# The second layer's MLP output as seven block products in place of eight (Strassen), for three quarters of its hidden width

## The chip, the cores and the metric

One core of one Trainium2 chip. The metric is the device time in microseconds of one execution, median of the runs shown.

## The reference

A decoder trunk of two layers, 512 tokens of width 1024, in float32. Each layer mixes tokens (three mixers fed by one input projection) and then channels. The change is in the channel mixing of the second layer and the final norm:

```python
h2 = rms_norm(x, norm2_w[l]) * (1.0 + sc2) + sh2
x = x + g2 * (jnp.square(jax.nn.relu(h2 @ w_up[l])) @ w_down[l])
...
return rms_norm(x, final_norm_w)
```

w_up is 1024 x 4096, w_down 4096 x 1024. g2 is one number per output column.

## The kernel before, in words

The residual x lies in eight tiles xt[m], 128 of the 1024 columns on the partitions, the 512 tokens along the free axis. A matrix product is made of three matmuls on values split in two (mm3, lines 199 to 201): high times high, and the two mixed products. A split (lines 192 and 193, 469 and 470) is a ScalarE cast to fp32r, the high part, and a VectorE subtraction, the low part.

The work is a list of jobs (class Job). A job computes output columns for all tokens in PSUM banks of 128x512 and is cut into pieces of four blocks of 128 rows of the weights. For a piece, emit_split (line 448) loads 128x1024 weights into raw by SP's queue and splits them into wH and wL; emit_mm (line 474) issues the matmuls with the weights' 128x128 blocks as the stationary operand and the activations, 128x512, as the moving one. A job of two output blocks has two pieces of 24 matmuls. At a job's end its evac reads the PSUM banks. run (line 513) puts the jobs in order: it splits the pieces ahead of the one in work (two held at a time) and adds up estimated times of TensorE and VectorE, by which it slips in the mixers' streams; in the second layer's MLP there are no streams. This order is that of the program text; buffers and the final order on each engine are worked out for the whole program when it is compiled, with splits and evacs marked as of high priority.

The MLP goes in four quarters qt of the hidden width. In each, four jobs up{qt}{mp} compute Relu and square (lines 1491, 1492) and split the result into uH and uL; then four jobs dn{qt}{mp} multiply by w_down, and evac_dn adds the result, times g2, to xt (line 1504). In the first quarter the first two up jobs are paired: their weights are kept and the tokens go in two halves of 256. In the last quarter the last two dn jobs are paired too. There, evac_dn also turns each xt[m] into token order (to_tokens, lines 1453 to 1458: a transpose on TensorE, a square with its sum on ScalarE, a product with the final norm's weight on VectorE) and, after the last block, final (lines 1461 to 1473) computes the factor of each token (rstd_cols, lines 360 to 368), scales and stores 256 KB for each half of the columns of 128 tokens.

Of the kernel before, what the change touches and what calls it, by code (L numbers as in the profile page):

```python
# [10 lines left out]
F32 = mybir.dt.float32  # L11
# [72 lines left out]
class Job:  # L84
# [11 lines left out]
    def pieces(self):  # L96
        return [Piece(self, k0, self.step, k0 == 0, k0 + self.step >= self.nk) for k0 in range(0, self.nk, self.step)]
# [9 lines left out]
def paired(fin, a, b):  # L107

    a.fin = b.fin = fin
    a.left = b.left = 2  # L110
    ps = a.pieces() + b.pieces()
    for p in ps:
        p.keep = True
    return [Unit(p, c) for c in HALVES for p in ps]

# [35 lines left out]
def tile_trunk(ctx: ExitStack, tc: tile.TileContext, io, out, depth=DEPTH):  # L151
# [7 lines left out]
    pa = ctx.enter_context(tc.tile_pool(name="pa", bufs=26))  # L159
# [7 lines left out]
    def tmp():  # L167
        return tf.tile([P, T], F32, name="tmp", tag="tmp")
# [13 lines left out]
    def tr_bank():  # L182
        return psp.tile([P, T], F32, name="tr", tag="tr", bufs=2)
# [53 lines left out]
    def fixed(n):  # L237
        used[0] += n
        return slab[:, used[0] - n:used[0]]
# [151 lines left out]
    class SumSq:  # L391
        def __init__(self):
            self.acc = None
            self.kept = {}
# [52 lines left out]

    def emit_split(p):
        j = p.job
        w = sum(n for _, n in j.cols)  # L450
# [23 lines left out]
    def emit_mm(u, ks):  # L474
        p, c = u.p, u.c
        j = p.job
        if j.ps is None:
            if j.pre is not None:
                j.pre()
            j.ps = [(j.bank[i] if j.bank else acc_bank)() for i in range(len(j.ms))]  # L480
# [32 lines left out]
    def run(items, ahead=2, step=2):  # L513
# [43 lines left out]
        while True:  # L557
# [56 lines left out]
            w = (u.c.stop - u.c.start) / T  # L614
# [27 lines left out]
    def layer(l, lys):  # L642
# [790 lines left out]

        w_up = io["w_up"][l].rearrange("(k p) c -> p k c", p=P)
        w_dn = io["w_down"][l].rearrange("(k p) c -> p k c", p=P)
        if last:
            xw = [pa.tile([P, 4, P], F32, name="xw", tag="pa") for _ in range(8)]
            sqs = fixed(32).rearrange("p (a b) -> p a b", a=4)
            s4 = fixed(4)
            r4 = fixed(4)  # L1440
            q4 = fixed(4)
            fwb = [pa.tile([P, T], F32, name="fwb", tag="pa") for _ in range(2)]
            for i in range(2):
                sync.dma_start(fwb[i], io["final_norm_w"][i * T:(i + 1) * T].rearrange("(o d) -> o d", o=1).broadcast_to([P, T]))
        else:
            yield Stream(fin, "next", ada(l + 1, "next", [2, 3, 0, 1, 4, 5, 8, 9, 6, 7, 10, 11], pa, "pa", 2.0))
        ss = SumSq()

        def to_tokens(m, c):
            tbs = range(c.start // P, c.stop // P)  # L1450
            pt = tr_bank()
            for tb in tbs:
                pe.transpose(pt[:, tb * P:(tb + 1) * P], xt[m][:, tb * P:(tb + 1) * P], ident)
            q = tmp()
            for tb in tbs:
                act.activation(q[:, tb * P:(tb + 1) * P], pt[:, tb * P:(tb + 1) * P], AF.Square,
                               accum_out=sqs[:, tb, m:m + 1])
                dve.tensor_mul(xw[2 * tb + m // 4][:, m % 4, :], pt[:, tb * P:(tb + 1) * P],
                               fwb[m // 4][:, m % 4 * P:(m % 4 + 1) * P])

        def final(c):
            t = slice(c.start // P, c.stop // P)
            s_, r_, q_ = s4[:, t], r4[:, t], q4[:, t]
            dve.tensor_reduce(out=s_, in_=sqs[:, t, :], op=ALU.add, axis=mybir.AxisListType.X)
            rstd_cols(s_, r_, q_)
            for tb in range(t.start, t.stop):
                for i in range(2):
                    o = xw[2 * tb + i]
                    if i:
                        act.activation(o, o, AF.Identity, scale=r4[:, tb:tb + 1])  # L1470
                    else:
                        dve.tensor_scalar(o, o, r4[:, tb:tb + 1], None, op0=ALU.mult)
                    sync.dma_start(o2[tb * P:(tb + 1) * P, i * T:(i + 1) * T], o.rearrange("p m c -> p (m c)"))

        def dn_pre():
            exp_ln_set()
            if not last:
                lys[l + 1] = begin(l + 1)
                scale_of(l + 1, lys[l + 1]["A1"], M_SC1, "norm1_w")

        for qt in range(4):
# [19 lines left out]
            for mp in range(4):  # L1501
                def evac_dn(i, ps, c=ALL, mp=mp, qt=qt):
                    m = 2 * mp + i
                    dve.scalar_tensor_tensor(xt[m][:, c], ps[:, c], mod[l][:, M_G2 + m:M_G2 + m + 1], xt[m][:, c],  # L1504
                                             op0=ALU.mult, op1=ALU.add)
                    if qt == 3:
                        if last:
                            to_tokens(m, c)
                            if m == NK - 1:
                                final(c)  # L1510
                        else:
                            ss.add(xt[m], c, m)
                            if m == NK - 1:
                                norm1(l + 1, lys[l + 1], ss, c)
# [5 lines left out]
                                 need=["next"] if end and not last else ["ada.11"], pre=dn_pre if end else None))  # L1520
# [79 lines left out]
```

## Time and profile before

| | us |
|---|---|
| median of three runs | 1988.61 (1986.53 to 1992.06) |
| the profiled execution | 1988.82 |
| its span, first to last instruction | 1987.1 |
| TensorE busy in the span | 1949.8 |
| VectorE busy | 1277.8 |
| ScalarE busy | 871.6 |

The engines are PE (TensorE's matmuls), PEld (its weight loads, which overlap them), DVE (VectorE), ACT (ScalarE), POOL (GpSimd) and SP (the queue that issues the DMAs). A busy time is the union of an engine's instructions; a matmul's end is modelled, so of matmuls the distance between starts counts. The second layer's MLP goes from about 1625 us to the end of the span.

### The profile page before, as it was taken

The page shows a single profiled execution, that of the slowest core. Times are in us where ns is not written, and L with a number is a line of the kernel's source. Part 1 is how long each engine was busy: PE and PEld are TensorE (multiplying, and loading weights), DVE is VectorE, ACT ScalarE, POOL GpSimd, SP SyncE. Part 2 cuts the span into 40 slices and gives each one's busy share as a digit, 9 for nine tenths or more (in the row PEclk, how much of TensorE's full clock was granted, in tenths as well). Part 3 has the DMA queues.
Part 4 walks back from the last instruction along what each step waited for, and adds up shares of the span by engine and source line. Part 5 has one row for each costly group of instructions (what it writes and reads, how often), then busy time and mean ns, then how long its engine had stood idle before and what let it go on. Part 6 is the DMA issues. An engine that isn't in the chain of part 4 may idle for free.

```text
span 1987.1 us, 26736 instructions
## 1 busy us (share of the span) xinstructions
PE 1949.8 (98%) x9940; PEld 1613.1 (81%) x9940; DVE 1277.8 (64%) x2368; ACT 871.6 (44%) x1562; POOL 94.9 (5%) x135
## 2 busy tenths in 40 slices
PE   7998999999999999999999999999999999999998
PEld 5787777788888988888897787778888898888887
DVE  4799768967846986333578985687575572333334
ACT  4453626733534534142545445384343354233243
POOL 0110210100000000000001101001000000000000
PEclk9999999999999999999999999999999999999999
DMA  9864353552444694333425433425233422333321
GB/s 288 222 168 131 107 153 108 156 188 87 136 127 142 223 371 161 95 103 98 118 86 139 113 103 90 118 70 151 67 104 108 156 95 96 96 96 96 95 96 43
DMA packets 249623, 258.30 MB, mean 130 GB/s; under 512 B 33828, under 2 KB 208212, under 8 KB 249492
## 3 DMA queue, kind: packets, MB, share of 16 engines
q1 hardware_dynamic: 248912, 256.45, 42.3%
q8 instruction: 78, 1.28, 0.3%
q14 instruction: 53, 0.43, 0.1%
q10 hardware_dynamic: 356, 0.14, 0.0%
q0 software_dynamic: 224, 0.00, 0.0%
HBM read 232.81 MB, written 6.42 MB: 120 GB/s over the span
## 4 chain that ended last, share of the span: by engine, by line
PE 89%; DVE 5%; DMA 2%; issue 1%; ACT 1%; POOL 1%; SPq 0%; ACTq 0%; POOLq 0%; DVEq 0%
PE acc L199 25%; PE acc L201 25%; PE acc L200 25%; PE qk L225 2%; PE po L1001 1%; PE tr L992 1%; DVE wL L470 1%; PE po L907 1%; PE tr L894 1%; DVE sc L823 1%; PE qk L1204 1%; DVE m L822 1%; DMA araw<-in_ada_w_dram 1%; PE po L201 1%; PE po L200 1%
## 5 line engine op out<-in xcount | busy, mean ns | idle before, releaser
L199 PE MATMUL acc<-aH,wH 128*128 128x512 f32 x1544 | 613.6, 398 | 10.6 <-DVE paL L193 5.3
L201 PE MATMUL acc<-aH,wL 128*128 128x512 f32 x1544 | 606.7, 393 | 0.9 <-DVE wL L470 0.8
L200 PE MATMUL acc<-aL,wH 128*128 128x512 f32 x1544 | 606.5, 393 | 0.0
L469 ACT CAST wH<-raw 128x1024 fp32r<-128x1024 f32 (+2 forms) x290 | 295.2, 1026 | 289.5 <-PE acc L200 250.5
L470 DVE TENSOR_TENSOR wL<-raw,wH 128x1024 fp32r<-128x1024 f32 (+2 forms) x290 | 343.3, 1199 | 16.0 <-ACT wH L469 8.3
L199 PEld LDWEIGHTS acc<-aH,wH 128*128 128x128 f32 x1544 | 291.4, 189 | 72.8 <-DVE paL L193 6.1
L201 PEld LDWEIGHTS acc<-aH,wL 128*128 128x128 f32 x1544 | 291.0, 188 | 62.5 <-DVE wL L470 2.1
L200 PEld LDWEIGHTS acc<-aL,wH 128*128 128x128 f32 x1544 | 291.6, 189 | 57.6 <-issue 0.7
L199 PE MATMUL acc<-uH,wH 128*128 128x512 f32 x448 | 174.9, 390 | 0.0
L201 PE MATMUL acc<-uH,wL 128*128 128x512 f32 x448 | 174.6, 390 | 0.0
L200 PE MATMUL acc<-uL,wH 128*128 128x512 f32 x448 | 174.3, 389 | 0.0
L193 DVE TENSOR_TENSOR uL<-tmp,uH 128x512 fp32r<-128x512 f32 x64 | 43.9, 691 | 189.2 <-ACT uH L192 189.2
L1491 ACT ACTIVATE tmp<-acc 128x512 f32<-128x512 f32 x60 | 35.3, 592 | 220.0 <-PE acc L201 220.0
L1504 DVE SCALAR_TENSOR_TENSOR x<-acc,slab,x 128x512 f32<-128x512 f32 (+1 forms) x64 | 43.8, 716 | 128.7 <-PE acc L201 128.7
L343 DVE SCALAR_TENSOR_TENSOR aacc<-araw,slab,aacc 128x512 f32<-128x512 f32 x140 | 104.0, 749 | 5.7 <-DMA araw<-in_ada_w_dram 4.1
L200 PEld LDWEIGHTS acc<-uL,wH 128*128 128x128 f32 x448 | 84.1, 188 | 17.4
L201 PEld LDWEIGHTS acc<-uH,wL 128*128 128x128 f32 x448 | 84.1, 188 | 17.4
L199 PEld LDWEIGHTS acc<-uH,wH 128*128 128x128 f32 x448 | 84.1, 188 | 17.1
L882 DVE TENSOR_TENSOR_SCAN tmp<-tmp 128x512 f32<-128x512 f32 (+1 forms) x64 | 52.5, 826 | 21.5 <-ACT tmp L875 21.4
L675 POOL TENSOR_TENSOR tmp<-tmp,slab 128x512 f32<-128x512 f32 (+1 forms) x20 | 31.6, 1581 | 719.5 <-DVE tmp L674 708.6
L1312 DVE SCALAR_TENSOR_TENSOR tmp<-tg,acc 128x512 f32<-128x512 f32 x16 | 11.0, 685 | 67.0 <-PE acc L201 67.0
L822 DVE MAX8 m<-sc 128x8 f32<-128x256 f32 (+2 forms) x96 | 52.8, 552 | 1.2 <-POOL sc L800 0.2
(307 smaller groups left out, 3022.1 us busy)
## 6 DMA issues: line engine op xcount, KB each, us to landing
araw<-in_ada_w_dram SPq DMA_DIRECT2D x192, 256.0 KB, 5.4
raw<-in_w_in_dram SPq DMA_DIRECT2D x96, 512.0 KB, 4.1
raw<-in_w_up_dram SPq DMA_DIRECT2D x64, 512.0 KB, 4.6
raw<-in_w_down_dram SPq DMA_DIRECT2D x64, 512.0 KB, 4.6
raw<-in_w_in_dram SPq DMA_DIRECT2D x56, 256.0 KB, 4.4
acb<-acd SPq DMA_DIRECT2D x32, 256.0 KB, 4.6
raw<-in_w_br_ssd_dram SPq DMA_DIRECT2D x16, 512.0 KB, 4.5
raw<-in_w_out_dram SPq DMA_DIRECT2D x16, 512.0 KB, 4.2
```

Source lines behind the costliest of these rows:

```text
L193: dve.tensor_sub(L, src, H)
L199: pe.matmul(ps, a[0], b[0], start=start, stop=False)
L200: pe.matmul(ps, a[0], b[1], start=False, stop=False)
L201: pe.matmul(ps, a[1], b[0], start=False, stop=stop)
L225: pe.matmul(ps, q[hh][:, cq], k[n][hh][:, ck], start=n == 0, stop=n == 1)
L343: dve.scalar_tensor_tensor(a, raw, cs[:, k:k + 1], a, op0=ALU.mult, op1=ALU.add)
L469: act.copy(H[:, :w], src)
L470: dve.tensor_sub(L[:, :w], src, H[:, :w])
L822: dve.max(out=m8, in_=sc[tb])
L882: dve.tensor_tensor_scan(out=nv, data0=nv, data1=nv, initial=1.0, op0=ALU.mult, op1=ALU.bypass)
L1491: act.activation(r, ps, AF.Relu)
L1504: dve.scalar_tensor_tensor(xt[m][:, c], ps[:, c], mod[l][:, M_G2 + m:M_G2 + m + 1], xt[m][:, c], op0=ALU.mult, op1=ALU.add)
```

## The change

The second layer's MLP gets a function of its own, last_mlp; the first layer keeps the old code. Its weights are now the moving operand: a class Rows, derived from Job, has pieces of two blocks of 128 rows and 512 columns, and an output tile is 128 tokens by 512 columns. The hidden width goes in four quarters of eight blocks, taken as four pairs (e = 0, 1).

In the first three quarters the product is made by blocks: the tokens in two halves of 256, the hidden blocks by e, the output columns in two halves d. Seven products (1, 2, 6, 7, 5, 4, 3 in this order) replace eight. The four weight quadrants R[e, d] (128x2048 each) are loaded by DMA during the quarter's up stage; their sums are made in place on VectorE (t3 during the up stage, t2, t1 and t4 ahead of their products), each over 128x1024. The sums of activations (S) are made by VectorE at the end of each pair of up blocks, and they and the plain blocks are split: seven tiles of 128x512 a pair. A product has two token tiles of four blocks, two pieces of 12 matmuls; its evac adds each PSUM bank to the accumulators y (product 1 to two of them, product 6 to one of these), by a ScalarE copy where an accumulator is new. y[1] to y[4] take the tag at, y[5] and y[7] the tag acb; both are kinds of buffers of the mixers, as are those of R (yH, yL), of the rows of g2 and the norm's weight (tg, cbt) and of xtok (x).

During the first quarter's up stage x is turned into token order (32 transposes, eight ScalarE copies) and stored; it is loaded again in the last quarter's up stage, where so_far(0) and so_far(1) combine the accumulators, multiply by g2 and add x, 13 VectorE operations of 128x512 each. behind is a ScalarE copy of one column that keeps a load from starting before something else is done.

The last quarter is plain: job p0 for the first 512 output columns, four token tiles at once; job p1 for the others, one token tile after another over weights that are kept split (in the buffers of h2), each with its evac, its final and its two stores.

```diff
@@ pool
-    pa = ctx.enter_context(tc.tile_pool(name="pa", bufs=26))
+    pa = ctx.enter_context(tc.tile_pool(name="pa", bufs=28))
@@ beside emit_split and emit_mm, which call these for a Rows job
+    def split_form(p):
+        j = p.job
+        src = j.form(p.k0 // 2)
+        if p.keep:
+            p.H, p.L = ([ap_.tile([P, T], F32R, name=n, tag=n) for _ in range(p.nk)] for n in ("aH", "aL"))
+            with tc.high_priority():
+                for k in range(p.nk):
+                    split(src[:, k * T:(k + 1) * T], p.H[k], p.L[k])
+            return
+        H, L = (wp.tile([P, 1024], F32R, name=n, tag=n)[:, :p.nk * T] for n in ("wH", "wL"))
+        with tc.high_priority():
+            split(src, H, L)
+        p.H, p.L = ([X[:, k * T:(k + 1) * T] for k in range(p.nk)] for X in (H, L))
+
+    def product(u):
...
+        for i in range(u.c.start, u.c.stop):
+            if i not in j.ps:
+                j.ps[i] = psp.tile([P, T], F32, name="dn", tag="dn", bufs=4)
+            for k in range(p.nk):
+                kk = p.k0 + k
+                a = [X[:, i * P:(i + 1) * P] for X in j.lhs(kk)]
+                mm3(j.ps[i], a, (p.H[k], p.L[k]), kk == 0, kk == j.nk - 1)
+            if p.last:
+                with tc.high_priority():
+                    j.evac(i, j.ps[i])
...
@@ last_mlp
+            def plus(key, i, src):
+                if (key, i) not in y:
+                    y[key, i] = at_whole() if key < 5 else tf.tile([P, T], F32, name="acb", tag="acb", bufs=6)
+                    act.copy(y[key, i], src)
+                else:
+                    dve.tensor_add(y[key, i], y[key, i], src)
...
+            def evac_plain(d):
+                def f(tb, ps):
+                    t = tmp()
+                    dve.tensor_mul(t, ps, rowb["g", d])
+                    dve.tensor_add(xf[tb, d], xf[tb, d], t)
+                    squares(tb, d)
+                    if d == 0:
+                        dve.tensor_mul(xf[tb, d], xf[tb, d], rowb["f", d])
+                    else:
+                        final(tb, d)
+                return f
...
+            for n in (4, 4, 4, 4):
+                first, end = g0 == 0, g0 + n == 16
...
+                        split(r1[:, 0:V], aH, aL)
+                        split(r2, bH, bL)
+                        dve.tensor_add(S[0], r1[:, V:], r2[:, V:])
+                        dve.tensor_sub(S[1], S[0], r1[:, 0:V])
+                        split(c_, cH, cL)
+                        dve.tensor_sub(S[2], r1[:, 0:V], r1[:, V:])
+                        dve.tensor_sub(S[3], r2[:, 0:V], S[1])
+                        split(d_, dH, dL)
...
+                def fetch(e, d, h, R=R, us=us, g0=g0, n=n):
...
+                    behind(R[e, d, h], us["r", 0, 0])
+                    sync.dma_start(r,
+                                   w_dn[:, e, g0 + 2 * h:g0 + 2 * h + k, d * T:(d + 1) * T])
+
+                def t3(h, R=R):
+                    dve.tensor_sub(R[0, 1, h], R[1, 1, h], R[0, 1, h])
+
+                def t2(h, R=R):
+                    dve.tensor_add(R[0, 0, h], R[0, 1, h], R[0, 0, h])
+                    return R[0, 0, h]
+
+                def t1(h, R=R):
+                    dve.tensor_sub(R[0, 1, h], R[1, 1, h], R[0, 0, h])
+                    return R[0, 1, h]
+
+                def t4(h, R=R):
+                    dve.tensor_sub(R[0, 0, h], R[1, 0, h], R[0, 0, h])
+                    return R[0, 0, h]
...
+                def evac_of(m):
+                    def f(i, ps):
+                        for a in {1: (1, 2), 6: (1,)}.get(m, (m,)):
+                            plus(a, i, ps)
+                    return f
...
+                prods = [(1, raw_(0, 0), "a11"), (2, raw_(1, 0), "a12"), (6, t2, "s2"), (7, raw_(0, 1), "s3"),
+                         (5, t1, "s1"), (4, t4, "a22"), (3, raw_(1, 1), "s4")]
+                yield from add([Rows(f"p{m}.{g0}", n, form, lhs(a), 2, evac_of(m)) for m, form, a in prods])
@@ layer
         if last:
...
+            yield from last_mlp()
+            return
```

## Rows read from the trace of the kernel before

**Rows 1.** The page's first lines: span, and busy us of each engine, its share.

```profile
span 1987.1 us, 26736 instructions
...
PE 1949.8 (98%) x9940; PEld 1613.1 (81%) x9940; DVE 1277.8 (64%) x2368; ACT 871.6 (44%) x1562; POOL 94.9 (5%) x135
```

**Rows 2.** Windows of the MLP: stretch, length, busy us by engine, clock, DMA.

```profile
core 0: us, PE busy (x) PEld busy (x) DVE busy (x) ACT busy (x) POOL busy (x), PEclk, DMA share, GB/s
...
1680.00:1720.00 40.00, 40.00 (x178) 33.14 (x177) 14.24 (x15) 5.28 (x5) 0.00 (x0) 1.00 0.37 117
1720.00:1760.00 40.00, 40.00 (x178) 33.10 (x178) 12.92 (x15) 20.98 (x33) 0.00 (x0) 1.00 0.26 81
```

**Rows 3.** Timeline of PE: start, us, instruction; two pieces begin here.

```profile
1683.78 0.39 PE L200 MATMUL acc<-uL,wH 128*128 128x512 f32 x1
...
1684.23 0.39 PE L199 MATMUL acc<-uH,wH 128*128 128x512 f32 x1
...
1689.44 0.39 PE L201 MATMUL acc<-uH,wL 128*128 128x512 f32 x1
1689.67 0.39 PE L199 MATMUL acc<-uH,wH 128*128 128x512 f32 x1
```

**Rows 4.** Timeline of PE: the last two half-width matmuls.

```profile
1976.94 0.28 PE L200 MATMUL qk<-uL,paH 128*128 128x256 f32 x1
1977.06 0.28 PE L201 MATMUL qk<-uH,paL 128*128 128x256 f32 x1
```

**Rows 5.** Timeline of all engines after the last matmul.

```profile
1977.42 0.48 DVE L1504 SCALAR_TENSOR_TENSOR x<-qk,slab,x 128x256 f32<-128x256 f32 x1
...
1979.76 0.16 DVE L1464 TENSOR_REDUCE slab<-slab 128x2 f32<-128x16 f32 x1
...
1981.42 1.33 ACT L1470 ACTIVATE xw<-xw,slab 128x512 f32<-128x512 f32 x2 [0.82 <-DVE slab L368]
...
1981.93 1.79 SPq L1473 DMA_DIRECT2D out_dram<-xw  x4
```

**Rows 6.** Timeline of DVE, a down stage: an evac of two banks, two subtractions.

```profile
1689.19 1.43 DVE L1504 SCALAR_TENSOR_TENSOR x<-acc,slab,x 128x512 f32<-128x512 f32 x2 [7.18 <-PE acc L201]
1690.54 2.35 DVE L470 TENSOR_TENSOR wL<-raw,wH 128x1024 fp32r<-128x1024 f32 x2
```

**Rows 7.** Timeline of DVE: two of 512 columns, one of 256, in SBUF.

```profile
1590.42 1.29 DVE L470 TENSOR_TENSOR paL<-raw,paH 128x512 fp32r<-128x512 f32 x2
...
1618.29 0.42 DVE L426 TENSOR_TENSOR tmp<-tmp 128x256 f32<-128x256 f32 x1
```

**Rows 8.** Instructions of tile wH: durations in ns, first and last start.

```profile
L200 PEld LDWEIGHTS acc<-uL,wH x224: 187/188/188, 1667.9 to 1951.0; 128*128 128x128 f32 x112
...
L469 ACT CAST wH<-raw x53: 1037/1049/1070, 1649.0 to 1932.7; 128x1024 fp32r<-128x1024 f32 x53
```

**Rows 9.** Windows of 100 us, columns as in rows 2.

```profile
100.00:200.00 100.00, 94.34 (x436) 76.24 (x436) 99.18 (x226) 48.02 (x80) 9.16 (x18) 0.97 0.53 149
300.00:400.00 100.00, 99.53 (x565) 77.76 (x564) 88.86 (x222) 70.95 (x171) 10.11 (x11) 1.00 0.42 133
...
700.00:800.00 100.00, 100.00 (x452) 82.81 (x451) 72.50 (x99) 39.13 (x56) 0.00 (x0) 1.00 0.74 252
```

**Rows 10.** Timeline of ACT: a cast, and the end of an up stage.

```profile
1684.20 1.05 ACT L469 CAST wH<-raw 128x1024 fp32r<-128x1024 f32 x1 [4.38 <-PE acc L200]
...
1754.47 0.60 ACT L1491 ACTIVATE tmp<-acc 128x512 f32<-128x512 f32 x1 [5.69 <-PE acc L201]
1754.96 1.04 ACT L469 CAST wH<-raw 128x1024 fp32r<-128x1024 f32 x1
...
1757.42 0.64 ACT L1492 ACTIVATE tmp<-tmp 128x512 f32<-128x512 f32 x1
```

**Rows 11.** Timeline of SP: up weights asked for during a down stage.

```profile
1673.59 40.32 SPq L457 DMA_DIRECT2D raw<-in_w_up_dram  x8
```

**Rows 12.** The page's DMA issues: tensors, count, size, us to landing.

```profile
raw<-in_w_down_dram SPq DMA_DIRECT2D x64, 512.0 KB, 4.6
```

More of the change, by code (lines that the diff above doesn't have):

```diff
@@ L96, in pieces @@
     def pieces(self):
-        return [Piece(self, k0, self.step, k0 == 0, k0 + self.step >= self.nk) for k0 in range(0, self.nk, self.step)]
+        return [Piece(self, k0, min(self.step, self.nk - k0), k0 == 0, k0 + self.step >= self.nk)
+                for k0 in range(0, self.nk, self.step)]
     def units(self, fin):
@@ L114, in paired, with __init__, units @@
     return [Unit(p, c) for c in HALVES for p in ps]
+class Rows(Job):
+    def __init__(self, name, nk, form, lhs, tiles, evac, by_parts=False, need=(), pre=None):
+        super().__init__(name, None, nk, [], range(tiles), None, evac, need=need, dve=0.65, pre=pre, step=2)
+        self.form, self.lhs, self.by_parts = form, lhs, by_parts
+        self.ps = None
+    def units(self, fin):
+        self.fin = fin
+        ps = self.pieces()
+        n = len(self.ms)
+        if not self.by_parts:
+            cs = [slice(0, n)]
+        else:
+            cs = [slice(i, i + 1) for i in range(n)]
+            for p in ps:
+                p.keep = True
+        self.left = len(cs)
+        return [Unit(p, c) for c in cs for p in ps]
 class Stream:
@@ L446, in add @@
                                      op0=ALU.add, op1=ALU.subtract)
+    def split_form(p):
[12 more added lines that the diff above has]
+    def product(u):
+        p = u.p
+        j = p.job
+        if j.ps is None:
+            if j.pre is not None:
+                j.pre()
+            j.ps = {}
+        for i in range(u.c.start, u.c.stop):
[8 more added lines that the diff above has]
+                    j.evac(i, j.ps[i])
+        p.left -= 1
+        if p.last:
+            j.left -= 1
+            if j.left == 0:
+                j.fin.add(j.name)
     def emit_split(p):
         j = p.job
+        if isinstance(j, Rows):
+            split_form(p)
+            return
         w = sum(n for _, n in j.cols)
@@ L476, in emit_mm @@
         j = p.job
+        if isinstance(j, Rows):
+            product(u)
+            return
         if j.ps is None:
@@ L613, in run @@
             ks = list(range(done_k, min(done_k + step, u.p.nk)))
-            w = (u.c.stop - u.c.start) / T
+            w = (u.c.stop - u.c.start) / (len(job.ms) if isinstance(job, Rows) else T)
             on_pe(0.66 * len(ks) * len(job.ms) * w)
@@ L1436, in layer @@
         if last:
[L1437 to L1446, printed above, removed]
@@ L1447, in layer @@
-        ss = SumSq()
[L1449 to L1473, printed above, removed]
+            yield from last_mlp()
@@ L1475, in dn_pre @@
+            return
+        yield Stream(fin, "next", ada(l + 1, "next", [2, 3, 0, 1, 4, 5, 8, 9, 6, 7, 10, 11], pa, "pa", 2.0))
+        ss = SumSq()
         def dn_pre():
             exp_ln_set()
-            if not last:
-                lys[l + 1] = begin(l + 1)
-                scale_of(l + 1, lys[l + 1]["A1"], M_SC1, "norm1_w")
+            lys[l + 1] = begin(l + 1)
+            scale_of(l + 1, lys[l + 1]["A1"], M_SC1, "norm1_w")
         for qt in range(4):
@@ L1506, in evac_dn @@
                     if qt == 3:
[L1507 to L1514, printed above, removed]
+                        ss.add(xt[m], c, m)
+                        if m == NK - 1:
+                            norm1(l + 1, lys[l + 1], ss, c)
                 end = qt == 3 and mp == 3
@@ L1519, in layer @@
                                  evac_dn, kbase=8 * qt, dve=1.3, each=qt == 3 and mp >= 2,
-                                 need=["next"] if end and not last else ["ada.11"], pre=dn_pre if end else None))
+                                 need=["next"] if end else ["ada.11"], pre=dn_pre if end else None))
             yield from add(downs[:2])
```

130 lines of the change are left out of this document (added).

## The prediction

> **What bounds the kernel now.** I read the page's busy shares first: the profiled execution spans 1987.1 us, and TensorE is busy in 1949.8 of them, VectorE in 64% [rows 1]. The windows of the second layer's MLP say it more sharply: in each 40 us TensorE is busy for 40.00, at the granted clock of 1.00 (its 2.4 GHz level), while VectorE is busy for 13 to 14 us [rows 2]. So nothing that only shortens VectorE's, ScalarE's or a DMA's work can help here, and whatever takes matmuls away helps as long as the others keep up. TensorE's own timeline gives the price of a matmul: one piece of weights (24 matmuls of 512 columns) runs from 1684.23 to the next piece's first matmul at 1689.67, 5.44 us, so 0.2267 us each; the 0.39 us shown for one overlaps its neighbours [rows 3]. The half-width matmuls of the last two jobs start 0.12 us apart [rows 4], so a pair of them costs 0.24.
>
> **The change, part by part.** Before, the second layer's products by w_down are 768 matmuls of 512 columns, or two halves for one. Afterwards each of the first three quarters has 7 products x 2 token tiles x 4 blocks of 128 x 3 = 168, and the last one 192: 696. The stationary operand is now an activation tile and the moving one a weight row block, but both keep their sizes (128x128 against 512 columns).
> 1. 72 matmuls fewer at 0.2267: **-16.3 us**.
> 2. The last quarter no longer runs two jobs in halves: 192 half-width matmuls at 0.12 were 23.0 us, the 96 full ones in their place take 21.8: **-1.2 us**.
> 3. The end. Before, the last matmul starts at 1977.06, the first output DMA is issued at 1981.93, four follow each other within 1.79 us, and the span ends at 1987.1: 10.0 us [rows 4, 5]. Now, after the last matmul: 0.36 until VectorE starts, a multiply from PSUM 0.72, an add 0.65, a square with its sum on ScalarE about 0.85, the same row of small operations 1.66 (from 1979.76 to 1981.42), a scaling 0.7: the first issue 0.1 or 0.2 us later than before, but two DMAs of 256 KB instead of four. At 0.45 us an issue that is **-0.8 us** net. The 32 transposes into token order move to the first quarter's up stage; TensorE pays the same for them there, and eight copies, eight stores and eight loads of 256 KB lie under matmuls.
> 4. VectorE. A subtraction over 1024 columns is 1.18 us of a pair's 2.35, an operation on PSUM over 512 is 0.72 of a pair's 1.43 [rows 6], over 512 in SBUF 0.65, over 256 0.42 [rows 7]. A Strassen quarter's product stage (168 x 0.2267 = 38.1 us) has 14 splits (16.5), 6 sums of weights in place (7.1) and, in quarters two and three, 16 additions out of PSUM (11.5): 35.1 us, 92% of the stage. In the first quarter 12 of the 16 are ScalarE copies: 26.5 us, 70%. Its up stage (43.5 us) has 8 splits (9.4), 4 pairs with three splits of 512, one of 256 and four sums of 256 (4.05 each, 16.2) and the two first sums (2.4): 28 us. What hides the 35.1 is the store of split weights: the last piece was cast at 1932.7 and its matmuls began some 5.4 us before the last of them, near 1951, so 13 us ahead [rows 8]. Where that cover is gone, see rival C. With cover, the price lies between a stretch with VectorE at 88.86%, where TensorE lost 0.47 us in 100, and one at 99.18%, where it lost 5.66 [rows 9]: for two stages of 38 us, 0.4 to 4.3. 92% is nearer to the first: **+2.0 us**.
> 5. The start of each Strassen product stage. The last up job's results used to be needed three quarters into the first job's second piece; now the first product wants them in its second piece, 2.72 us in, and 0.68 later for the last block. In the trace the first Relu starts at 1754.47, a weight cast is put between, and the second square ends at 1758.06 [rows 10]; a cast of 256 columns and a subtraction, 0.42 each if a cast is no slower than VectorE's operation of that width [rows 7], follow: 4.4 us after that Relu, against the 3.9 that the next job's start (four pitches after the matmul that released the Relu 0.42 before it, so 1754.96) plus 3.40 allows. That is 0.5 us late with the cast between, nothing without it, and 1.7 if a split of 1.18 stands in VectorE's queue too: three times 0 to 1.7. I take 0.5 each: **+1.5 us**.
> 6. What costs nothing. The loads are 32 of 512 KB, as before, but all in the up stages: 8 MB in 43.5 us, about 193 GB/s; the windows show 252 GB/s with TensorE busy for 100.00 of 100 [rows 9], and a load lands 4.6 us after its issue, the up weights being asked for up to eight pieces early [rows 11, 12]. Twelve further loads of 256 KB in the last up stage make some 265 GB/s there. The one-column ScalarE copies that hold the loads back wait for the first up job or for the last product; behind them stand casts of pieces that are already several ahead, and on SP's queue the next up weights. The additions of a product wait on VectorE for TensorE, and the next splits queue behind them: that is in term 4. ScalarE has 14 casts and 12 copies at most, about 22 of 38 us. The last quarter's up stage has 26 more VectorE operations (17 us) on 9.4 + 5.2: covered.
>
> Sum: -16.3 - 1.2 - 0.8 + 2.0 + 1.5 = -14.8. The profiled execution took 1988.82 us (its span and 1.7 around it), 0.2 above the median of the three runs, so **1974.0**. With the ends of terms 4 and 5 (0.4 and 0; 4.3 and 5.1) this case reaches from 1970.9 to 1979.9.
>
> **Rivals.** A, the forecast: TensorE stays the bound.
> B, the splits hang on the additions. VectorE works in order, and an addition waits for a product's last matmul with splits behind it. If a third of the sums and additions (10.0 us in the first quarter, 18.6 in each of the others, 47.2) stands between a cast and the matmul that waits, 15.7 us are lost and the time is 1988.8 - 18.3 + 15.7 = 1986.2, no change that can be told. For it: 92% in the stage. Against it: 63 of 81.6 us over a whole quarter, and the pieces stored ahead.
> C, the other side. The product stage holds 28 activation tiles, the weights' four tiles of 2048 columns and twelve sums at once, so room for split pieces may shrink to two. A piece now lasts 12 matmuls, 2.72 us; a cast starts 0.42 after its buffer's last reader (1683.78 to 1684.20), takes 1.05, and the subtraction 1.18 [rows 3, 10, 6]: 2.65, with next to nothing to spare, and every sum or addition that falls between is TensorE's loss. All of it would be 1988.8 - 18.3 + 47.2 = 2017.7; slower by over 0.3% from (18.3 + 6.0) / 47.2 = 51% on. The Trainium skill, Perfetto Trace Analysis, Optimization Strategy, says that the same gap repeating on the engine that should be saturated can mean too little SBUF or PSUM for the next tile; no such gap stands in the rows of this stage.
> D, the other 1640 us move. Buffers and order are worked out for the whole program at once, and one pool is given two buffers more and PSUM a new kind of tile, so the order may change before the MLP too. A second stretch like that of 100 to 200 us, where 5.66 were lost, or two of them: 1980 to 1985; it may also gain as much.
> E, a matmul less is worth less than its pitch, if the tiles' exchange shows the weight load instead: at 0.188 [rows 8] 72 give 13.5, and the time is 1976.8. The trace holds 0.2267 in every piece of both kinds. The Trainium skill, TensorE: Matmul & The Clock Gate, Back-to-back issue gap, gives about 131 ns for a sustained matmul of 512 columns; by that the 72 would be worth 9.4 us, and the time 1980.9. This case's rows disagree with it (226.7 ns).
>
> **How the numbers follow.** Chances: A 0.67, B 0.14, C 0.08, D 0.08, E 0.03. About 0.3%, 6 us, is what a measurement of this kernel can tell from no change. Faster: A, E, half of D and the mildest of B, 0.76; the same: most of B and some of D, 0.15; slower: C and a little of D, 0.09. The range goes from 1966 (A's best end and a gain of D's kind) to 1988 (B), which leaves out C and the edges of D, about 0.14.
>
> **What would show it.** TensorE's busy time lower by some 16 us; its windows from 1640 us on still full, with at most a pause of a microsecond where each product stage starts; matmuls of the new products 0.227 apart; VectorE near 90% in the second and third product stage, with subtractions done before TensorE asks. Wrong would be: TensorE waiting again and again for a split's subtraction (B, C), a later start of the MLP than now (D), or another pitch (E).

## The result and the profile after

The changed kernel takes 1969.59 us (median of 5, 1969.02 to 1972.04) against 1989.05 for the kernel before on the same chip (median of 5), a ratio of 0.9900 with a 95% interval of 0.9883 to 0.9916. In two later sessions the same program took 1972.71 and 1973.87 us, ratios 0.9922 (0.9907 to 0.9938) and 0.9919 (0.9903 to 0.9935); the second is the median of five runs, without a sixth, slow execution of 4609.47 us. The gain by these medians is 15.6 to 19.5 us. The forecast was 14.8, with a time of 1974.0 us in a range of 1966 to 1988 us.

The page's first lines, of the profiled execution of 1969.26 us:

```profile
span 1967.5 us, 26644 instructions
...
PE 1931.2 (98%) x9773; PEld 1593.6 (81%) x9773; DVE 1376.7 (70%) x2508; ACT 909.7 (46%) x1625; POOL 93.7 (5%) x135
```

Against [rows 1], TensorE is busy for 18.6 us less, VectorE for 98.9 more. Windows of the four product stages, in the columns of [rows 2]; the first three are the Strassen quarters, the last is plain:

```profile
1670.05:1708.12 38.07, 38.07 (x169) 31.53 (x168) 27.61 (x31) 23.15 (x33) 0.00 (x0) 1.00 0.09 28
1751.64:1790.14 38.50, 38.50 (x170) 31.54 (x169) 33.15 (x42) 18.69 (x23) 0.00 (x0) 1.00 0.03 9
1833.66:1872.14 38.48, 38.38 (x170) 31.45 (x168) 36.13 (x47) 18.23 (x27) 0.00 (x0) 1.00 0.04 10
1915.66:1959.30 43.64, 43.64 (x193) 35.85 (x191) 22.20 (x45) 13.77 (x32) 0.00 (x0) 1.00 0.07 25
```

168 matmuls at 0.2267 are 38.08 us. The first stage takes just that, the next two 0.42 and 0.40 more, with VectorE busy for 73, 86 and 94% of the stage. A pause that the window still counts as busy shows only in the starts of the matmuls. The timeline of the second Strassen stage, ScalarE (ACT), VectorE (DVE) and TensorE (PE) in order of time; line 216 is the cast, 217 the subtraction, 1551 an addition out of PSUM, 1656 the sum t4, 1605 and 1606 the Relu and the square of an up job's bank (here the two of the last up job):

```profile
1751.16 0.60 ACT L1605 ACTIVATE tmp<-acc 128x512 f32<-128x512 f32 x1 [3.65 <-PE acc L225]
...
1751.66 1.04 ACT L216 CAST wH<-rd 128x1024 fp32r<-128x1024 f32 x1
...
1752.60 0.63 ACT L1606 ACTIVATE tmp<-tmp 128x512 f32<-128x512 f32 x1
...
1753.13 0.59 ACT L1605 ACTIVATE tmp<-acc 128x512 f32<-128x512 f32 x1
1753.61 0.40 ACT L216 CAST paA<-tmp 128x256 fp32r<-128x256 f32 x1
...
1753.90 0.64 ACT L1606 ACTIVATE tmp<-tmp 128x512 f32<-128x512 f32 x1
...
1754.04 0.43 DVE L217 TENSOR_TENSOR paA<-tmp,paA 128x256 fp32r<-128x256 f32 x1 [2.00 <-ACT paA L216]
...
1755.05 0.39 PE L223 MATMUL dn<-wH,paA 128*128 128x512 f32 x1
...
1759.65 1.22 DVE L217 TENSOR_TENSOR wL<-rd,wH 128x1024 fp32r<-128x1024 f32 x1
...
1775.35 2.35 DVE L1656 TENSOR_TENSOR rd<-rd 128x1024 f32<-128x1024 f32 x2
...
1776.67 4.08 ACT L216 CAST wH<-rd 128x1024 fp32r<-128x1024 f32 x4 [2.64 <-DVE rd L1656]
...
1777.68 0.69 DVE L1551 TENSOR_TENSOR acb<-acb,dn 128x512 f32<-128x512 f32 x1
1778.29 1.22 DVE L217 TENSOR_TENSOR wL<-rd,wH 128x1024 fp32r<-128x1024 f32 x1
...
1778.85 0.61 PE L223 MATMUL dn<-wH,paH 128*128 128x512 f32 x2
1779.30 0.27 PE L1517 MATMUL tr<-slab 128*8 128x128 f32 x1
1779.56 0.50 PE L224 MATMUL dn<-wL,paH 128*128 128x512 f32 x1
```

At the start of the stage the last activation split that product 1 needs is done at 1754.47 (1754.04 and 0.43) and wanted at 1755.05: no wait. Twenty-seven us in, the first piece of product 4 starts at 1778.85; its subtraction stands behind the two sums t4 and an addition, and ends at 1779.51; only then, at 1779.56, can the first matmul on the low part start. The third stage has the same pause at the same place, and neither stage has another.

The timeline after the last matmul, where [rows 5] is its answer of before:

```profile
1958.95 0.39 PE L225 MATMUL dn<-aH,paL 128*128 128x512 f32 x1
1959.38 0.69 DVE L1587 TENSOR_TENSOR tmp<-dn,rowb 128x512 f32<-128x512 f32 x1 [0.86 <-PE dn L225]
1960.10 0.69 DVE L1588 TENSOR_TENSOR acb<-acb,tmp 128x512 f32<-128x512 f32 x1
...
1963.20 0.72 ACT L1567 ACTIVATE at<-at,slab 128x512 f32<-128x512 f32 x1 [0.80 <-DVE slab L392]
...
1963.95 0.33 SPq L1568 DMA_DIRECT2D out_dram<-at  x1
1964.37 0.38 SPq L1568 DMA_DIRECT2D out_dram<-acb  x1
```

From the last matmul's start to the end of the span it is 8.6 us now, 10.0 before.

The start of the second layer's last output projection ahead of the MLP, in the kernel before and in the changed one:

```profile
1604.83 0.28 PE L199 MATMUL qk<-aH,paH 128*128 128x256 f32 x1
...
1603.56 0.28 PE L223 MATMUL qk<-aH,paH 128*128 128x256 f32 x1
```

The two profiled executions differ by 19.56 us: 1.27 because this projection starts earlier, 16.84 from there to the last matmul, 1.46 behind it. The experiments ask what each of the three is.

### The profile page after: what moved, and what is told of

Read it like the earlier page. It is cut to its first block, busy times and chain, and to the rows that moved or that the text cites. A ratio compares the mean times of both kernels' runs of the same rounds, so it can differ in the third digit from the quotient of the medians.

```text
span 1967.5 us, 26644 instructions
## 1 busy us (share of the span) xinstructions
PE 1931.2 (98%) x9773; PEld 1593.6 (81%) x9773; DVE 1376.7 (70%) x2508; ACT 909.7 (46%) x1625; POOL 93.7 (5%) x135
## 4 chain that ended last, share of the span: by engine, by line
PE 87%; DVE 7%; DMA 3%; issue 1%; ACT 1%; POOL 1%; SPq 0%; ACTq 0%; POOLq 0%; DVEq 0%
PE acc L223 22%; PE acc L225 22%; PE acc L224 22%; PE dn L224 3%; PE dn L225 3%; PE dn L223 3%; PE qk L249 2%; DVE wL L534 1%; PE po L1068 1%; DMA araw<-in_ada_w_dram 1%; PE tr L1059 1%; DVE sc L890 1%; DVE m L889 1%; DVE tmp L949 1%; PE po L974 1%
## 5 line engine op out<-in xcount | busy, mean ns | idle before, releaser
L533 ACT CAST wH<-raw 128x1024 fp32r<-128x1024 f32 (+2 forms) x262 | 266.5, 1023 | 225.9 <-PE acc L224 177.2
L534 DVE TENSOR_TENSOR wL<-raw,wH 128x1024 fp32r<-128x1024 f32 (+2 forms) x262 | 311.4, 1198 | 22.9 <-ACT wH L533 15.1
L223 PE MATMUL acc<-uH,wH 128*128 128x512 f32 x224 | 87.7, 392 | 0.0
L225 PE MATMUL acc<-uH,wL 128*128 128x512 f32 x224 | 87.2, 389 | 0.0
L224 PE MATMUL acc<-uL,wH 128*128 128x512 f32 x224 | 87.1, 389 | 0.0
L224 PE MATMUL dn<-wL,paH 128*128 128x512 f32 x176 | 68.7, 390 | 0.1
L225 PE MATMUL dn<-wH,paL 128*128 128x512 f32 x176 | 68.5, 389 | 0.0
L223 PE MATMUL dn<-wH,paH 128*128 128x512 f32 x176 | 68.1, 389 | 0.0
L217 DVE TENSOR_TENSOR wL<-rd,wH 128x1024 fp32r<-128x1024 f32 x46 | 55.6, 1219 | 2.6 <-ACT wH L216 2.6
L216 ACT CAST wH<-rd 128x1024 fp32r<-128x1024 f32 x46 | 47.0, 1048 | 19.4 <-DVE rd L1652 14.0
```

Of the source, the lines that this page charges most:

```text
L216: act.copy(H, src)
L217: dve.tensor_sub(L, src, H)
L223: pe.matmul(ps, a[0], b[0], start=start, stop=False)
L224: pe.matmul(ps, a[0], b[1], start=False, stop=False)
L225: pe.matmul(ps, a[1], b[0], start=False, stop=stop)
L533: act.copy(H[:, :w], src)
```

## The experiments

The stretch from the first down matmul to the last, with three up stages in it, separates the changed MLP from what lies ahead. In the changed kernel it goes from 1670.05 to 1958.95, 288.9 us. Where an experiment's first down matmul is called late, that is against 1670.05.

**e1_eight: eight products in the changed layout.** The up jobs take the plain activations, the sums go, and the first three quarters multiply as the last one does. (Not shown: the loads come in the last quarter's order, and five additions that combine accumulators go.)

```diff
-                        if end:
+                        if True:
                             u = us["u", mp, i] = hl()
...
-                        if m in (5, 7) and not end:
-                            yield lambda h=(m - 5) // 2, t3=t3: t3(h)
...
+                if not end:
+                    half_ = [(0, 0), (1, 0), (0, 1), (1, 1)]
+                    yield from add([Rows(f"p{d}.{g0}", 8, lambda m, d=d, R=R: R[half_[m][0], d, half_[m][1]],
+                                         lambda kk, us=us: us["u", 2 * half_[kk // 2][1] + kk % 2, half_[kk // 2][0]], 4,
+                                         evac_sum(d)) for d in range(2)])
+                    g0 += n
+                    continue
```

> The changed kernel with its layout, its loads and its tail, but eight block products in each of the first three quarters for seven: 72 matmuls more, no sums of weights or of activations, and ScalarE copies or VectorE additions of each bank into the accumulators only at the end of two jobs. If the gain is 72 matmuls at their pitch and the sums lie under them, TensorE is full here too: 72 x 0.2267 = 16.3 us more matmuls, less the 0.7 of pauses that the changed kernel has left, so 1969.3 + 15.6 = 1984.9 us, and from the MLP's first matmul to the last 371.0 us for 355.4. If most of the gain is the layout's (fewer half-width pairs, a shorter end, another order before the MLP), the time stays under 1977. If a matmul less is worth less than its pitch (131 ns), 1969.3 + 9.4 = 1978.7.

Measured: 1988.11 us (median of 12), ratio 0.9988 (0.9978 to 0.9997). Windows of its first three product stages:

```profile
1676.38:1719.90 43.52, 43.52 (x193) 36.05 (x192) 10.65 (x10) 14.69 (x21) 0.00 (x0) 1.00 0.12 36
1763.42:1806.94 43.52, 43.52 (x193) 36.05 (x192) 14.53 (x17) 13.00 (x16) 0.00 (x0) 1.00 0.04 12
1850.46:1893.98 43.52, 43.52 (x193) 36.05 (x192) 14.53 (x17) 14.01 (x28) 0.00 (x0) 1.00 0.04 11
```

From the first down matmul to the last it takes 304.57 us, 15.66 more than with seven products, where 15.6 was expected. The time is 3 us above the 1984.9 expected; its first down matmul came 6.3 us late, in a part that scatters (e8_again). From its last output projection (1609.90) to the last matmul it takes 371.05 us, 1.18 less than the 372.23 of the kernel before: that is the layout, with eight products in both. So almost all of the gain is the exchange of eight products for seven, at the full pitch. With the 0.66 us of pauses that e7_nosums measures, the 72 matmuls were 16.3 us, which is 226.7 ns each. Rival E, a matmul worth less than its pitch, is out. The Trainium skill (TensorE: Matmul & The Clock Gate, Back-to-back issue gap) gives about 131 ns for a sustained 512-column matmul, by which the 72 would be 9.4 us, an estimate. This run disagrees with it (226.7 ns).

**e7_nosums: no sums of weights in the product stages.**

```diff
                 def t2(h, R=R):
-                    dve.tensor_add(R[0, 0, h], R[0, 1, h], R[0, 0, h])
                     return R[0, 0, h]
```

and the same for t1 and t4.

> The six sums of weights in place (t2, t1, t4) of each Strassen product stage are left out, the products take the quadrants as they stand: 7.1 us of VectorE's work less in each of three stages, the same matmuls. If the sums lie under the matmuls but for the pauses that the changed kernel shows (0.8 us in all, both at the tenth piece of a stage), 0.7 us less: some 1968.9, and 288.1 to 288.3 us from the first down matmul to the last for 288.9. If the additions and sums cost the 3.5 us of terms 4 and 5 of the prediction in some other form, 1966.

Measured: 288.25 us from the first down matmul to the last, 0.66 less, and each Strassen stage 38.08 us long:

```profile
1676.37:1714.45 38.08, 38.08 (x170) 31.53 (x168) 22.39 (x26) 23.14 (x33) 0.00 (x0) 1.00 0.09 28
1757.97:1796.05 38.08, 38.08 (x170) 31.53 (x168) 28.23 (x37) 18.79 (x23) 0.00 (x0) 1.00 0.03 9
1839.57:1877.65 38.08, 38.08 (x170) 31.53 (x168) 31.41 (x42) 18.19 (x27) 0.00 (x0) 1.00 0.04 11
```

The time of 1972.09 us, ratio 0.9918 (0.9904 to 0.9933), cannot show so small a difference, and this execution's MLP began late. (The two fuller stages are 0.82 shorter, but a small transpose that stood in a pause now costs 0.16 elsewhere.) The pauses are the sums' whole price: eighteen sums, of which 14.9 us of VectorE's work fell into the three stages (82.0 us busy for 96.9) and the rest into the up stages ahead of them, cost TensorE 0.66. (The place that the expectation calls the tenth piece is the one after ten pieces, the first of product 4.)

**e2_more6 and e6_inplace: how much room VectorE has left.** Both add six operations of 1.2 us to each Strassen stage, the first into a tile that nobody reads, the second without a new tile:

```diff
+                def more(h, R=R):
+                    for _ in range(1):
+                        t = wp.tile([P, 1024], F32, name="more", tag="more", bufs=1)
+                        dve.tensor_sub(t, R[0, 1, h], R[0, 0, h])
...
                     dve.tensor_add(R[0, 0, h], R[0, 1, h], R[0, 0, h])
+                    more(h)
```

```diff
                     dve.tensor_add(R[0, 0, h], R[0, 1, h], R[0, 0, h])
+                    dve.tensor_sub(R[1, 0, h], R[1, 1, h], R[1, 0, h])
```

and the same behind the sums of t1 and t4.

> The changed kernel with six further subtractions of 128x1024 on VectorE in each of the three Strassen product stages, two with each pair of sums of weights, into a tile that nobody reads: 7.1 us a stage. VectorE's work in the stages of 38.1 us would be 34.7, 40.3 and 43.2 us for the 27.6, 33.2 and 36.1 it has now. Theory that VectorE stands at the brink and nothing is stored ahead: the work beyond 38.1 is TensorE's loss, 0 + 2.2 + 5.1 = 7 us, so about 1976 us, more (up to 1984) if the six also come between a cast and the matmul that waits. Rival, that split pieces stored ahead cover the stage (13 us deep, as the prediction had it): under 1.5 us, 1970 to 1971.

> The six further operations of 1.18 us in each Strassen product stage again, but done in place on a weight quadrant that is not read in between (R[1,1] - R[1,0] twice gives it back; after product 4 it is dead), so that no tile is added. If VectorE's room in the stage is what costs time, the stages are as in e2_more6 (38.4, 43.1 and 43.8 us from first to last matmul, for 37.9, 38.3 and 38.3), from the first down matmul to the last 299 to 301 us for 288.9, and with the first down matmul near 1670 the time is 1980 to 1982. Rival, that the pauses in e2_more6 came from its other addresses: 289 to 291, and 1970 to 1972.

Measured: e2_more6 2002.82 us, ratio 1.0062 (1.0047 to 1.0078); e6_inplace 1987.35, ratio 0.9991 (0.9981 to 1.0000). In e2_more6 only 11.0 of some 30 us more lie in the MLP (299.89 us from the first down matmul to the last), where 7 to 15 were expected; its first down matmul came at 1694.73, 24.7 late. The next experiment takes that up. In e6_inplace the first down matmul is at 1672.35, and the added time is in the MLP: 304.53 us, 15.6 more, where 10 to 12 were expected. The windows of its second and third Strassen stages, and of 2.8 us in the second:

```profile
1754.81:1800.59 45.78, 41.44 (x170) 32.22 (x169) 40.18 (x48) 18.43 (x23) 0.00 (x0) 0.96 0.03 7
...
1844.11:1890.07 45.96, 41.60 (x170) 32.09 (x169) 42.25 (x52) 18.15 (x26) 0.00 (x0) 0.96 0.04 10
...
1785.00:1787.80 2.80, 2.80 (x8) 2.14 (x7) 2.23 (x3) 0.00 (x0) 0.00 (x0) 0.50 0.03 6
```

And TensorE's timeline just ahead of that:

```profile
1782.07 0.73 PE L223 MATMUL dn<-wH,paH 128*128 128x512 f32 x2 [0.86 <-ACT wH L216]
...
1784.34 0.53 PE L223 MATMUL dn<-wH,paH 128*128 128x512 f32 x1 [1.54 <-ACT wH L216]
```

VectorE is busy for 40.2 and 42.2 us, 2.1 and 4.2 more than the 38.1 that the matmuls need, and the stages are 7.7 and 7.9 us longer than that. TensorE pauses up to 1.9 us at a time. In the MLP eleven of its waits, 7.7 us, are for a cast, and the casts ahead of the long pauses wait for a sum; two, 1.3 us, are for a split's subtraction. After several such pauses its granted clock was 0.50, the 1.2 GHz level, for eight matmuls in the second stage and six in the third (0.43 us apart), which is 1.6 and 1.2 us more; the expectation lacked these. So VectorE's work beyond the stage accounts for 2.1 and 4.2 us and the clock for 1.6 and 1.2. The other 4.0 and 2.5 us, in which VectorE too stood idle, were not taken apart; that they come from the order in which the engines wait for each other is likely but not shown. The theory that nothing much is stored ahead holds, and the rival, that a store of pieces would cover 7 us more, is out: six operations added cost 4.8 to 7.5 us in each of the two fuller stages, and under 1 us in the first.

**e5_small6: the extra tile without its work.** As e2_more6, each write 8 columns wide:

```diff
-                        dve.tensor_sub(t, R[0, 1, h], R[0, 0, h])
+                        dve.tensor_sub(t[:, 0:8], R[0, 1, h][:, 0:8], R[0, 0, h][:, 0:8])
```

> The kernel of e2_more6 (six writes of an unread tile of 128x1024 in each Strassen product stage), each write only 8 columns wide, some 0.1 us: the tile's place in memory stays, the work goes. In e2_more6 the MLP's first down matmul started at 1694.73 us, 24.7 later than in the changed kernel (1670.05), before any of the added work. Theory that the extra tile gives all tiles of the program other addresses, and that these make other waits and stretches at a lower granted clock ahead of the MLP (the prediction's rival D): first down matmul again some 20 to 25 us late, from there to the last matmul 288.9 to 290 as in the changed kernel, some 1991 us in all. Rival, that the added work delayed it by the order of the program: first down matmul within 3 us of 1670, and 1970 us.

Measured: 1990.84 us (median of 12), ratio 1.0001 (0.9987 to 1.0015): the whole gain is gone with next to no work added, as expected. First down matmul at 1689.48, 19.4 late (13 to 19 behind the kernels that e8_again compares); from there to the last 289.61, 0.7 longer. One of the places ahead of the MLP, the norm of the first layer's MLP; SP, ScalarE and TensorE of e5_small6:

```profile
639.66 6.57 SPq L521 DMA_DIRECT2D raw<-in_w_up_dram  x2
...
643.53 1.05 ACT L533 CAST wH<-raw 128x1024 fp32r<-128x1024 f32 x1 [2.72 <-DMA raw<-in_w_up_dram]
644.48 0.72 ACT L430 ACTIVATE tmp<-x 128x256 f32<-128x256 f32 x2
...
647.16 0.70 PE L444 MATMUL qk<-tmp,slab 128*128 128x256 f32 x2 [2.91 <-DVE tmp L434]
```

The same work in the changed kernel:

```profile
621.93 18.34 SPq L521 DMA_DIRECT2D raw<-in_w_up_dram  x2
...
634.80 1.03 ACT L533 CAST wH<-raw 128x1024 fp32r<-128x1024 f32 x1
...
641.26 0.64 PE L444 MATMUL qk<-tmp,slab 128*128 128x256 f32 x2
```

The first of the two loads of w_up in the first row is issued at 639.66 instead of 621.93: between 631 and 640 us SP's queue waited 5.0 us for an older load of raw and 3.4 for the last reader of a tile tmp, whose place the new one seems to take. In the changed kernel the queue waits for the same two (6.4 and 11.5 us), but ahead of the second of these loads and not the first. SP's queue is 9 us behind already at the load of w_out before (620.85 for 611.81); why was not taken apart. The cast waits for the load, the norm's squares stand behind the cast on ScalarE, and TensorE waits 2.9 us for them. In the 20 us from 660 on its granted clock was 0.91 on top, 1.00 in the changed kernel's window from 655 to 675. About a third of the 19 us arises between 641 and 657; the rest comes in smaller steps up to 1610. This is rival D as a mechanism, and its price, up to 24.7 us in e2_more6, was set too low at 11.

**e3_bufs2: split pieces in two buffers.**

```diff
-        H, L = (wp.tile([P, 1024], F32R, name=n, tag=n)[:, :p.nk * T] for n in ("wH", "wL"))
+        H, L = (wp.tile([P, 1024], F32R, name=n, tag=n, bufs=2)[:, :p.nk * T] for n in ("vH", "vL"))
```

> The changed kernel with the split pieces of the products held in only two buffers (a kind of their own), so that a piece of 12 matmuls (2.72 us) must be cast and subtracted while the one before it is multiplied. Rival C of the prediction: 2.65 us of cast and subtraction leave no room, and each sum or addition between them is TensorE's loss, up to 47.2 us; with half of it 1969.3 + 24 = 1993 us, and pauses of TensorE at most pieces. Against it, if a depth of two is enough, because the subtractions end only 0 to 2 us before TensorE wants them in the changed kernel anyway: under 3 us, to 1972.

Measured: 1984.11 us, ratio 0.9966 (0.9955 to 0.9977), but again mostly ahead of the MLP (first down matmul at 1681.84, 11.8 late). From there to the last down matmul it takes 290.24 us, 2.0 more than without pauses. Expected were 1993 us or at most 1972; the MLP is as the second case has it. In the program's order, made anew for this kernel, some matmuls of the next up stage stand between those of the products (11 and 12 among the down matmuls of the second and third stage) and fill what would be pauses. So rival C's chain of 2.65 against 2.72 us per piece is met by another order, and costs 1.3 us beyond the changed kernel, not 47.

**e4_together: the last job's four token tiles at once.**

```diff
-                                             evac_plain(d), by_parts=d == 1, pre=exp_ln_set if d else None)])
+                                             evac_plain(d), by_parts=False, pre=exp_ln_set if d else None)])
```

> The changed kernel with the last job p1 taken with its four token tiles at once in place of one after another, so that all four evacs, squares and stores come behind the last matmul. The end from the last matmul's start (8.55 us) then has four multiplies from PSUM (0.72), four additions (0.65) on VectorE, four squares, four rows of small operations, and eight stores: 4 x 1.4 for 1.4, and some more for the small operations of four tiles: 7 to 10 us more, 1976 to 1979. If the stores' landing sets the end and not the evac, 3 us more.

Measured: 1974.90 us, ratio 0.9926 (0.9910 to 0.9941); from the last matmul to the end 11.96 us for 8.6. That is 3.4 more, near the expectation's second case of 3 and not 7 to 10: the last piece goes through the token tiles one after another, six matmuls (1.4 us) each, so the first two evacs and half of the third still run beside matmuls. The stores are then what is late: eight issues, the last pair from 1968.28 on. Ahead of the down matmuls this kernel is the changed one in its order.

**e8_again and e10_change: the changed kernel twice more.**

> The changed kernel as it is, once more, for how far the part ahead of the MLP moves between runs of the same program: first down matmul within 1.5 us of 1670.05, from there to the last matmul 288.9 within 0.1, the end 8.6, 1969 to 1971 us. If the 1.3 us by which the changed kernel reached its MLP earlier than the kernel before is the change's, it stays at 1668 to 1671; if it is the run's, it may be anywhere up to 1674.

> The changed kernel a third time, on the same chip as e10_deeper. If the ratio to the kernel before differs between sessions by more than its intervals (0.9900 and 0.9922 so far), here anything from 0.989 to 0.993; first down matmul between 1668 and 1675, and 288.9 us from there to the last.

Measured: 1972.71 and 1973.87 us. From the first down matmul to the last 288.93 and 288.95, the end 8.6, as expected; the first down matmul at 1672.67, outside the 1.5 us expected, and 1674.37. The last output projection ahead of the MLP starts at 1606.18 and 1607.89, at 1605.00 in e4_together and at 1603.56 in the first profile: four executions of the same order ahead of the MLP scatter over 4.3 us, with the kernel before (1604.83) among them. With e1_eight and e7_nosums (1609.90 and 1609.88), which differ from it in the MLP alone, it is 6.3. The 1.27 us cannot be told from this scatter.

**e9_deeper and e10_deeper: a deeper pool of weights.**

```diff
-    wp = ctx.enter_context(tc.tile_pool(name="wp", bufs=2))
+    wp = ctx.enter_context(tc.tile_pool(name="wp", bufs=3))
```

> The changed kernel with three instead of two buffers as the starting number of the pool of raw and split weights (raw, wH, wL), for the whole program: a deeper store of split pieces, and other addresses for all tiles. In the MLP it can give back at most the pauses that are left, 0.7 us: 288.2 to 288.9 us from the first down matmul to the last. Ahead of the MLP, if the extra tile of e5_small6 cost its 19 us by loads that wait for a buffer, more buffers for the loads bring the first down matmul to 1665 to 1670 for 1670.05 to 1672.67, and the time to 1962 to 1970. If the cost comes from where tiles lie and not from how many a kind may have, the addresses change here too, and the first down matmul comes 5 to 20 us later: 1975 to 1990.

> e9_deeper again, beside the changed kernel. If its deeper pool is worth what its profile showed, 0.7 us in the MLP and some 2 to 4 us before it, 2 to 6 us less than e10_change, and again 288.25 us from the first down matmul to the last. If its 1966.95 was the session's, the two are within 1.5 us.

Measured: 1966.95 us, ratio 0.9886 (0.9869 to 0.9903), and 1967.31, ratio 0.9888 (0.9872 to 0.9905), beside 1973.87 for the changed kernel on the same chip. This version beats both kernels. The windows of its Strassen stages (e9_deeper):

```profile
1668.20:1706.28 38.08, 38.08 (x170) 31.54 (x168) 27.24 (x30) 23.46 (x33) 0.00 (x0) 1.00 0.05 16
1749.80:1787.88 38.08, 38.08 (x170) 31.54 (x168) 33.78 (x41) 18.05 (x22) 0.00 (x0) 1.00 0.05 15
1831.40:1869.48 38.08, 38.08 (x170) 31.54 (x168) 36.50 (x47) 18.07 (x23) 0.00 (x0) 1.00 0.05 15
```

VectorE has as much to do (96% of the third stage), yet no pause is left: 288.25 us from the first down matmul to the last in both runs. The first down matmul comes at 1668.20 and 1668.64, where the three profiles of the changed kernel have 1670.05 to 1674.37. Nearly all of the gain ahead of the MLP arises in one place, in the second layer's mixers. The same 36 matmuls in e10_change, with the one that waits, and in e10_deeper:

```profile
1131.54 0.79 PE L223 MATMUL acc<-aH,wH 128*128 128x512 f32 x1 [3.98 <-DVE ysbL L978]
...
1124.67:1140.02 15.35, 11.37 (x37) 8.72 (x36) 15.25 (x41) 4.57 (x7) 0.47 (x1) 0.78 0.44 121
...
1126.02:1134.19 8.17, 8.17 (x37) 6.71 (x36) 8.10 (x24) 3.55 (x7) 0.29 (x1) 1.00 0.39 98
```

In the changed kernel TensorE waits 4 us there for VectorE, and its granted clock over the stretch is 0.78; with the deeper pool the order is another, there is no wait, and the stretch is 7.2 us shorter. The kernel before has this wait too (3.9 us). So it is not the loads that the expectation had in mind. Whether the number of buffers or the other order that came with it removes the wait was not taken apart.

## Why the prediction was right, and where its steps were off

**Terms 1 and 2** (-16.3 and -1.2) came out as put: from the last output projection to the last matmul the gain is 16.84, and with the 0.66 us of pauses given back 17.50. The pitch of 0.2267 and the count of matmuls carried the forecast; e1_eight shows each of the two alone (16.3 and 1.18).

**Term 3** (-0.8) was mis-sized; it measured -1.46. Its path to the first issue was right: 5.00 us after the last matmul's start, for 4.87 before. The issues take 0.8 us instead of 1.8, as reckoned. What it left out is that the last store also lands sooner: from the end of the last issue to the end of the span 2.8 us, where the four of before took 3.4.

**Term 4** (+2.0) and **term 5** (+1.5) were mis-sized: together 3.5, measured 0.66. In term 5 the wrong step was to put the split behind the second square. The weights' cast does stand where it was put, behind the first Relu (1751.16, 1751.66). But the part of the split that product 1 needs reads the first bank alone: its cast (1753.61) goes ahead of the second square (1753.90), and it is done 3.3 us after the first Relu, for 4.4 reckoned and 3.9 allowed. So it is ready 0.6 us early. In term 4 the amount of work was near (33.2 and 36.1 us in the fuller stages, for 35.1 forecast), but in part by luck: two of the splits and most of t2 fall into the up stage ahead, and splits and sums of the last up block, about 4 us, fall into the product stage, with one or two splits of the next up weights and, in the third, some 4 us of so_far. The 0.66 lies within the bounds of 0.4 to 4.3; the value between was chosen from a stretch of other work, and too high. Its reason does not hold either: "What hides the 35.1 is the store of split weights ... 13 us ahead". In the changed kernel a subtraction such as that of 1759.65 ends 1.7 us before its piece starts (1762.53), and the one of 1778.29 comes too late; from the fourth piece of a fuller stage to the tenth it is 0.7 to 1.8 us. What hides the work is that it is less than the stage and that its order on VectorE is near that in which TensorE asks; e6_inplace shows the cover gone with 7 us more.

**The rivals.** B (splits behind additions) has the right mechanism, and the one pause left in each fuller stage is its kind, together 0.66 us of the 15.7 it was given. C fell: two buffers cost 1.3 us in the MLP. E fell with e1_eight. D did not happen in the change itself, though it could have: a tile added by e5_small6 cost 13 to 19 us ahead of the MLP. Its chance of 0.08 was for a case that three of the experiments' kernels (e2_more6, e3_bufs2, e5_small6) then showed, and its price was an underestimate. That the two added buffers and the new tiles of the change left the time ahead alone was not something that the profile of before could show.

The forecast is thus right in its main terms. The profiled pair differs from it by 4.8 us: 2.8 of stalls that did not come, 0.7 at the end, and 1.3 ahead of the MLP, which is within the scatter. The two later medians lie closer to 1974.0 than the terms deserve: there the scatter ahead of the MLP hides what terms 4 and 5 had too much.

## What to carry to other kernels

Where one engine is full, a change that takes instructions from it is worth their count times the distance between their starts, as long as each other engine's work in the same stage stays below the stage: VectorE's work at up to 94% of the stage cost 0.7 us over three stages, and 7 us more of it cost 5 to 7.5 in each of the two fuller ones. Judge an experiment by the stretch that it is about and not by the whole time alone: in a program whose buffers are laid out as a whole, one more tile moved another part by 13 to 19 us, and one program alone scatters by 4 to 6 us ahead of the stretch. Try the depth of the weights' pool too: one buffer more took a further 6.6 us beside the changed kernel, most of it at a wait that the kernel before has as well. What it would give that kernel was not run.

## What the runs showed beyond what was expected

A tile that is hardly written cost 13 to 19 us in another part of the program; about a third of it arises where a load comes late because it waits for an older load and for the last reader of another tile (e5_small6). Pauses of TensorE cost more than their length: in e6_inplace a granted clock of 0.50 followed several of them, with matmuls 0.43 us apart; in e5_small6 the clock was 0.91 in the 20 us that begin 13 us behind a pause of 2.9, and in e10_change it was 0.78 over a stretch of 15.35 us with a wait of 4.0. In e2_more6, with pauses of up to 2.1 us in the same stages, no window of a product stage was below 1.00, so pauses alone don't say when it falls; that stays open.
